# Start addresses in SBUF: y's parts and sums 64 bytes further on, Strassen's weights at offset 0, and w1's chunk behind a Strassen chunk at its usual place

## The chip, the cores and the metric

The kernel runs on one core of one Trainium2 chip. The metric is the device time of one execution in microseconds (us). Three executions of the kernel before took 2162.35, 2159.93 and 2165.89 us; the median is 2162.35 us.

## What is computed

A two-layer transformer on 256 tokens of width 2048, in float32. Layer 0 mixes with stick-breaking attention, layer 1 with a sparse attention of three branches; behind each stands an MLP with a squared ReLU. The parts that matter here:

```python
def sqrelu_mlp(h, w1, w2):
    return jnp.square(jax.nn.relu(h @ w1)) @ w2

def reference(x, ...):
    h = x
    for layer in range(DEPTH):                       # DEPTH = 2
        ...
        h = h + stick_breaking_attention(rms_norm(h, ...), sb_w_qkv[slot], sb_w_out[slot])   # layer 0
        h = h + native_sparse_attention(rms_norm(h, ...), nsa_w_in[slot], ...)               # layer 1
        h = h + sqrelu_mlp(rms_norm(h, mlp_norm_g[layer]), mlp_w1[layer], mlp_w2[layer])
```

`mlp_w1` is 2048 x 8192 and `mlp_w2` 8192 x 2048 in each layer.

## The kernel before, in words

**Arithmetic.** Every large product is made in float32r on TensorE, with each operand split into a high part (ScalarE, a copy that rounds) and a low part (VectorE, the difference). A product is the sum of three matmuls: high by high, low by high, high by low. A matmul has a stationary operand (128 x 128, loaded by a weight load that runs beside the matmul before it) and a moving operand of 256 or 512 columns.

**Three kinds of chunk.** Weights come from HBM in chunks of 128 x 1024 numbers.

- `chunk_T` (line 194) makes a transposed product for w1 and for q and k. Stationary: the weights. Moving: x, 256 columns. A chunk is 16 matmuls with the high weights (`acc<-xs,hi`, x's high and low part in turn) and 8 with the low weights (`acc<-xs,lo`), all at line 208.
- `chunk_N` (line 155) makes a product with tokens as rows: v, the attentions' outputs, part of w2. Stationary: x or y (y is the MLP's hidden layer, or the attention's result). Moving: the weights, 512 columns. A chunk is 12 matmuls at line 159.
- `chunk_S` (line 239) does a part of w2 by Strassen's scheme: 21 matmuls with 256 columns at line 275 in the place of 12 with 512. Stationary: y or its sums `ss`. Moving: three plain blocks of the weights (`shi`, `slo`) and four sums of blocks (`hi`, `lo` out of `ts`).

**Order.** In `mlp` the hidden layer is cut into four parts (`fg` 0 to 3). For each part `group1` (line 440) runs 4 x 8 = 32 chunks of w1, and `group2` (line 468) the chunks of w2 that take this part in. In `group1` of `fg` 1 to 3 the last output block of the part before is done by eight Strassen chunks, two in every eight w1 chunks: `then={2: step, 5: step}` puts one behind the third and one behind the sixth. `group2` has eight Strassen chunks of its own between its `chunk_N`. With two layers, there are 6 groups of the first kind with 8 Strassen chunks each, so 48 of these, and 8 groups of the second kind with 64 Strassen chunks. TensorE takes its instructions in the order in which the code makes them.

**Places.** Below, the *place* of an operand is its start address within a partition, modulo 256 bytes. By the built program's memory map the buffers of x's parts, y's parts, `ss`, the weights' `hi` and `lo` and Strassen's `shi` and `slo` all begin at place 128, and every slice that a matmul takes out of them is a multiple of 256 bytes further on. The code adds an offset (line 131, counted in 4-byte numbers) to some of them: `NEAR` 0, `FAR` 16, `TURN` 8, `SUM` 48, `SUM0` 60. That gives:

| operand | role | offset | place |
|---|---|---|---|
| x, in `chunk_T` | moving | none | 128 |
| w1, q, k weights, usual | stationary | FAR | 192 |
| w1 at the start of `group1` for `fg` > 0, all 24 matmuls | stationary | TURN | 160 |
| w1 in the chunk behind a Strassen chunk: first 14 matmuls, then 2 + 8 | stationary | TURN, then FAR | 160, then 192 |
| y, `ss` | stationary | none | 128 |
| weights in `chunk_N` | moving | NEAR | 128 |
| Strassen's `slo`, `hi`, `lo`; in `group1` `shi` too | moving | SUM | 64 |
| Strassen's `shi` in `group2` (first 6 matmuls) | moving | SUM0 | 112 |

The chunk behind a Strassen chunk is split by `split_turn` (line 181): ScalarE and VectorE each do it in two instructions (896 and 128 columns) that write to different offsets, where the usual `split` (line 133) takes one each.

Of the kernel before, what the change touches and what calls it, by code (L numbers as in the profile page):

```python
# [8 lines left out]
F32 = mybir.dt.float32  # L9
F32R = mybir.dt.float32r  # L10
AF = mybir.ActivationFunctionType
OP = mybir.AluOpType
# [3 lines left out]
P = 128  # L16
T = 256
NT = T // P
D = 2048
KD = D // P  # L20
NB = 512
# [4 lines left out]
KC = 2  # L26
# [15 lines left out]
def hybrid_kernel(  # L42
# [6 lines left out]
    nc = tc.nc  # L49
    cpool = ctx.enter_context(tc.tile_pool(name="cpool", bufs=1))  # L50
# [3 lines left out]
    whi = ctx.enter_context(tc.tile_pool(name="whi", bufs=4))  # L54
    wlo = ctx.enter_context(tc.tile_pool(name="wlo", bufs=4))
# [5 lines left out]
    h = cpool.tile([P, NT, D], F32, name="h")  # L61
    xs = cpool.tile([P, KD, 2, T], F32R, name="xs")
    xhi, xlo = xs[:, :, 0, :], xs[:, :, 1, :]
    yhi = cpool.tile([P, KD, T], F32R, name="yhi")
    ylo = cpool.tile([P, KD, T], F32R, name="ylo")


    G_SB, G_M0, G_M1, G_NSA, G_Q, G_K = 0, KD, 2 * KD, 3 * KD, 64, 65
# [39 lines left out]
    def pump():  # L108
        if beside:
            b = beside[0]  # L110
            b[2] += b[1] / KC
            while b[2] >= 1:
                b[2] -= 1
                y = next(b[0], b)
                if y is b:
                    beside.remove(b)
                if y:
                    break
# [8 lines left out]

    PAD = 64  # L130
    NEAR, FAR, TURN, SUM, SUM0 = 0, 16, 8, 48, 60

    def split(raw, o=(NEAR, NEAR)):
        n = KC * NB
        view = lambda t, a: t[:, a:a + n].rearrange("p (k n) -> p k n", k=raw.shape[1])
        hi = view(whi.tile([P, n + PAD], F32R, tag="hi", name="hi"), o[0])
        nc.scalar.activation(hi, raw, AF.Copy)  # L137
        lo = view(wlo.tile([P, n + PAD], F32R, tag="lo", name="lo"), o[1])
        nc.vector.tensor_tensor(lo, raw, hi.bitcast(F32), op=OP.subtract)  # L139
        return hi, lo  # L140

    def load(src, k0, nk, n0, nn):
        raw = wraw.tile([P, nk, nn], F32, tag="raw", name="raw")
        nc.sync.dma_start(
            raw, src[k0 * P:(k0 + nk) * P, n0:n0 + nn].rearrange("(k p) n -> p k n", p=P)
        )
        return raw

    def load_split(*where, o=(NEAR, NEAR)):
        return split(load(*where), o)  # L150
# [3 lines left out]

    def chunk_N(ps, src, k0, n0, first, last, ahi, alo, koff=0, by_token=False):

        hi, lo = src if isinstance(src, tuple) else load_split(src, k0, KC, n0, NB)
        tiles = [(kk, k0 - koff + kk, t) for kk in range(KC) for t in range(NT)]
        mm = lambda a, b, k, t, s, e: nc.tensor.matmul(ps[t], a[:, k, t * P:(t + 1) * P], b, start=s, stop=e)  # L159
        if by_token:  # L160

            half = [slice(0, NB // 2), slice(NB // 2, NB)]
            for t, c in [(0, slice(0, NB)), (1, half[0]), (1, half[1])]:
                for a, w in ((ahi, hi), (alo, hi), (ahi, lo)):
                    for kk in range(KC):
                        k = k0 - koff + kk
                        nc.tensor.matmul(
                            ps[t][:, c], a[:, k, t * P:(t + 1) * P], w[:, kk, c], start=False, stop=True,
                            skip_group_check=True,
                        )  # L170
            return
        for part in [tiles]:
            for kk, k, t in part:
                mm(ahi, hi[:, kk, :], k, t, first and kk == 0, False)
                mm(alo, hi[:, kk, :], k, t, False, False)
            pump()
            for kk, k, t in part:
                mm(ahi, lo[:, kk, :], k, t, False, last and kk == KC - 1)
            pump()

    def split_turn(raw):

        flat = raw.rearrange("p k n -> p (k n)")
        n, c = KC * NB, KC * NB - P
        h, l = whi.tile([P, n + PAD], F32R, tag="hi", name="hi"), wlo.tile([P, n + PAD], F32R, tag="lo", name="lo")
        for a, b, o in ((0, c, TURN), (c, n, FAR)):
            nc.scalar.activation(h[:, o + a:o + b], flat[:, a:b], AF.Copy)
            nc.vector.tensor_tensor(
                l[:, FAR + a:FAR + b], flat[:, a:b], h[:, o + a:o + b].bitcast(F32), op=OP.subtract
            )  # L190
        cut = lambda t, o: [t[:, o(j) + j * P:o(j) + (j + 1) * P] for j in range(n // P)]
        return cut(h, lambda j: TURN if (j + 1) * P <= c else FAR), cut(l, lambda j: FAR)

    def chunk_T(ps, src, k0, n0, first, last, nk=KC, o=(FAR, FAR)):

        nm = KC * NB // P // nk
        tiles = [(kk, m) for kk in range(nk) for m in range(nm)]
        if o is None:
            hi, lo = split_turn(load(src, k0, nk, n0, nm * P))
        else:  # L200
            hi, lo = [
                [w[:, kk, m * P:(m + 1) * P] for kk, m in tiles]
                for w in (src if isinstance(src, tuple) else load_split(src, k0, nk, n0, nm * P, o=o))
            ]

        def mm(w, x, kk, m, s, e):
            o = ps[m // 2][:, (m % 2) * T:(m % 2 + 1) * T]
            nc.tensor.matmul(o, w, x[:, k0 + kk, :], start=s, stop=e, skip_group_check=True)  # L208

        for (kk, m), w in zip(tiles, hi):  # L210
            mm(w, xhi, kk, m, first and kk == 0 and m % 2 == 0, False)
            mm(w, xlo, kk, m, False, False)
        pump()
        for (kk, m), w in zip(tiles, lo):
            mm(w, xhi, kk, m, False, last and kk == nk - 1)
        pump()

    def proj_T(ps, src, n0, nk=KC, turn=False, then={}):

        for i in range(KD // nk):  # L220
            k0 = i * nk
            o = (TURN, TURN) if turn and i == 0 else None if i - 1 in then else (FAR, FAR)
            chunk_T(ps, src, k0, n0, k0 == 0, k0 + nk == KD, nk, o)
            if i in then:
                then[i]()

    def proj_Th(src, n0):

        ps = bank(acc, "acc")
        proj_T([ps], src, n0, 2 * KC)  # L230
        return ps
# [7 lines left out]
    def chunk_S(ps, src, k0, n0, first, last, ahi, alo, shi, slo, koff=0, o=SUM0):  # L239
# [9 lines left out]
        hi, lo = [  # L249
            wsum.tile([P, 3 * W + PAD], F32R, tag=n, name=n, bufs=1)[:, a:a + 3 * W]  # L250
            for n, a in (("shi", o), ("slo", SUM))
# [57 lines left out]
    def proj_N(src, n0, pool=acc, tag="acc"):  # L309
        ps = [bank(pool, tag) for _ in range(NT)]  # L310
        for k0 in range(0, KD, KC):
            chunk_N(ps, src, k0, n0, k0 == 0, k0 + KC == KD, xhi, xlo)
        return ps
# [87 lines left out]
    def out_proj(src, layer, g0):  # L401

        ps = {nb: [bank(acc, "acc") for _ in range(NT)] for nb in (0, 1)}
        for nb in (0, 1):
            for k0 in range(0, KD - HG, KC):
                chunk_N(ps[nb], src, k0, nb * NB, k0 == 0, False, yhi, ylo)
        drain()
        for nb in range(D // NB):
            if nb < 2:
                k00 = KD - HG  # L410
            else:
                ps[nb] = [bank(acc, "acc") for _ in range(NT)]
                k00 = 0
            for k0 in range(k00, KD, KC):
                chunk_N(ps[nb], src, k0, nb * NB, k0 == 0, k0 + KC == KD, yhi, ylo)
            add_h(nb, ps[nb])
            spawn(next_x(layer, nb, g0), 1)

    def mlp(l, layer, junk, done, last=None):
        w1, w2 = mlp_w1[l], mlp_w2[l]  # L420
        ss = junk.tile([P, 2, KD // 2, 4, P], F32R, name="ss", bufs=1)
        row = junk.tile([P, T], F32, name="row", bufs=1)

        def rows():
# [271 lines left out]
    with tc.tile_pool(name="m0p", bufs=2) as mp:  # L696
        wsum = mp
        def done0(nb, pool):
            spawn(next_x("nsa", nb, G_NSA, pool), 1.5)

        mlp(0, "m0", mp, done0)
# [5 lines left out]
    with tc.tile_pool(name="nsa", bufs=2) as ap, ExitStack() as last:  # L707
# [298 lines left out]
        for k0 in range(0, KD, GK):  # L1006
            raw = load(w_in, k0, GK, D + 6 * NB + GATES - P, P)
# [6 lines left out]
            for kk in range(GK):  # L1014
                k = k0 + kk
# [40 lines left out]
        for g in range(G):  # L1056
            ps = [bank(acc, "acc") for _ in range(NT)]
            for k0 in range(0, KD, KC):
                raw = wraw.tile([P, KC, NB], F32, tag="raw", name="raw")
# [26 lines left out]
    with tc.tile_pool(name="m1p", bufs=2) as mp:  # L1086
        wsum = mp
        ov = out[0].rearrange("(t p) d -> p t d", p=P)

        def done1(nb, pool):  # L1090
            if nb < D // NB - 1:
                nc.sync.dma_start(ov[:, :, nb * NB:(nb + 1) * NB], h[:, :, nb * NB:(nb + 1) * NB])

        mlp(1, "m1", mp, done1, ov)
# [29 lines left out]
```

## Time and profile before

| | |
|---|---|
| median of three executions | 2162.35 us |
| the profiled execution, its own time | 2154.16 us |
| its span, first to last instruction | 2152.4 us |
| granted TensorE clock | 1.000 |
| VectorE busy, ScalarE busy | 1597.2 us, 1205.3 us |

The profile's groups list a kind of instruction by line and operands, with its count and mean duration. A matmul's duration there is that of one from its start to its modelled end; since matmuls are pipelined, these overlap, and the mean says little about the rate. The rate is read from the timeline: it merges equal instructions in a row into one line with the start of the first and their count, so the difference of two starts, divided by the count, is what one matmul costs.

### The profile page before, as it was taken

Reading aid. Unit: us, or ns where it says so; the run is one execution under the profiler, and the core shown is the slowest. Engines: PE = TensorE matmul, PEld = TensorE weight load, DVE = VectorE, ACT = ScalarE, POOL = GpSimd, SP = SyncE. Lnnn points to the kernel's source line nnn. Section 1 sums busy time; section 2 is a strip of 40 time slices with the busy share of each in tenths; the row PEclk is TensorE's granted clock in tenths of the full one; section 3 lists DMA queues with packets and bytes.
Section 4 is the critical chain, followed back from the end, with each engine's and each line's share of the span. In section 5 each row is a group of like instructions: output and inputs, shape, how many; then the busy total and the mean of one; then the engine's idle time right before and its main releaser. Section 6 shows DMA issues by size and latency. Waiting matters only on the chain.

```text
span 2152.4 us, 37355 instructions
## 1 busy us (share of the span) xinstructions
PE 2145.5 (100%) x14898; PEld 1983.1 (92%) x14898; DVE 1597.2 (74%) x2241; ACT 1205.3 (56%) x1639; POOL 42.6 (2%) x75
## 2 busy tenths in 40 slices
PE   9999999999999999999999999999999999999999
PEld 9999988998998999999898888889989989989998
DVE  5556556568878878878877888755778798788786
ACT  6555665555555555555556666654555555555553
POOL 0000000000000000000000011000000000000000
PEclk9999999999999999999999999999999999999999
DMA  7655555665665665765667654456656656656664
GB/s 240 210 168 176 158 181 177 184 201 188 206 195 187 206 196 187 225 195 184 202 178 225 173 144 135 145 168 188 193 196 199 194 188 215 199 183 206 196 198 164
DMA packets 260790, 406.35 MB, mean 189 GB/s; under 512 B 13188, under 2 KB 91912, under 8 KB 260616
## 3 DMA queue, kind: packets, MB, share of 16 engines
q1 hardware_dynamic: 259800, 403.52, 60.1%
q8 instruction: 116, 1.90, 0.3%
q14 instruction: 58, 0.48, 0.1%
q10 hardware_dynamic: 816, 0.46, 0.1%
HBM read 401.83 MB, written 2.10 MB: 188 GB/s over the span
## 4 chain that ended last, share of the span: by engine, by line
PE 99%; DVE 0%; POOL 0%; ACT 0%; issue 0%; DVEq 0%; ACTq 0%; POOLq 0%
PE acc L208 43%; PE acc L159 37%; PE att L275 13%; PE att L159 1%; PE att L332 1%; PE att L946 1%; PE att L612 0%; PE att L660 0%; PE att L884 0%; PE att L940 0%; PE att L886 0%; PE att L885 0%; PE att L939 0%; PE att L938 0%; PE att L862 0%; PE att L779 0%
## 5 line engine op out<-in xcount | busy, mean ns | idle before, releaser
L137 ACT ACTIVATE hi<-raw 128x1024 fp32r<-128x1024 f32 x591 | 624.7, 1059 | 509.2 <-PE acc L208 211.3
L139 DVE TENSOR_TENSOR lo<-raw,hi 128x1024 fp32r<-128x1024 f32 x591 | 719.7, 1221 | 244.9 <-ACT hi L137 227.0
L208 PE MATMUL acc<-xs,hi 128*128 128x256 f32 x5360 | 669.0, 277 | 0.0
L208 PEld LDWEIGHTS acc<-xs,hi 128*128 128x128 f32 x5360 | 638.7, 188 | 1.0
L208 PE MATMUL acc<-xs,lo 128*128 128x256 f32 x2680 | 359.6, 277 | 0.0
L208 PEld LDWEIGHTS acc<-xs,lo 128*128 128x128 f32 x2680 | 329.4, 188 | 0.0
L159 PE MATMUL acc<-hi,yhi 128*128 128x512 f32 x828 | 324.6, 392 | 0.0
L159 PE MATMUL acc<-hi,ylo 128*128 128x512 f32 x828 | 323.0, 390 | 0.0
L159 PE MATMUL acc<-lo,yhi 128*128 128x512 f32 x828 | 223.3, 391 | 0.0
L137 ACT ACTIVATE hi<-ts 128x1024 fp32r<-128x1024 f32 x112 | 118.8, 1061 | 178.5 <-DVE ts L255 98.0
L159 PEld LDWEIGHTS acc<-lo,yhi 128*128 128x128 f32 x828 | 154.6, 188 | 31.5
L159 PEld LDWEIGHTS acc<-hi,ylo 128*128 128x128 f32 x828 | 155.5, 188 | 29.6 <-DVE ylo L319 0.2
L159 PEld LDWEIGHTS acc<-hi,yhi 128*128 128x128 f32 x828 | 155.5, 188 | 29.6 <-ACT yhi L318 0.2
L159 PE MATMUL acc<-hi,xs 128*128 128x512 f32 x704 | 177.5, 392 | 0.0
L248 DVE TENSOR_TENSOR ts<-raw 128x512 f32<-128x512 f32 x112 | 77.1, 691 | 128.2 <-DMA raw<-in_mlp_w_dram 128.0
L159 PEld LDWEIGHTS acc<-hi,xs 128*128 128x128 f32 x704 | 130.1, 188 | 26.5 <-ACT hi L137 0.2
L139 DVE TENSOR_TENSOR lo<-ts,hi 128x1024 fp32r<-128x1024 f32 x112 | 136.6, 1220 | 9.4 <-ACT hi L137 9.0
L253 ACT ACTIVATE shi<-raw 128x768 fp32r<-128x768 f32 x112 | 94.5, 844 | 60.8 <-PE att L275 36.3
L256 DVE TENSOR_TENSOR slo<-raw,shi 128x768 fp32r<-128x768 f32 x112 | 106.6, 952 | 0.4 <-PE att L275 0.4
L159 PE MATMUL acc<-lo,xs 128*128 128x512 f32 x352 | 96.7, 395 | 0.0
L275 PE MATMUL att<-hi,ss 128*128 128x256 f32 x672 | 95.9, 279 | 0.0
L275 PEld LDWEIGHTS att<-hi,ss 128*128 128x128 f32 x672 | 86.4, 189 | 0.0
(251 smaller groups left out, 2246.0 us busy)
## 6 DMA issues: line engine op xcount, KB each, us to landing
raw<-in_mlp_w_dram SPq DMA_DIRECT2D x512, 512.0 KB, 4.4
raw<-in_sb_w_qkv_dram SPq DMA_DIRECT2D x95, 512.0 KB, 4.3
raw<-in_nsa_w_in_dram SPq DMA_DIRECT2D x50, 512.0 KB, 3.8
raw<-in_sb_w_out_dram SPq DMA_DIRECT2D x32, 512.0 KB, 3.9
raw<-in_nsa_w_in_dram SPq DMA_DIRECT2D x64, 256.0 KB, 3.4
raw<-in_nsa_w_out_dram SPq DMA_DIRECT2D x32, 512.0 KB, 3.6
w1t<-in_nsa_cmp_w_dram SPq DMA_DIRECT2D x8, 512.0 KB, 3.9
h<-in_x_dram SPq DMA_DIRECT2D x8, 256.0 KB, 4.4
```

The source lines that it names most:

```text
L137: nc.scalar.activation(hi, raw, AF.Copy)
L139: nc.vector.tensor_tensor(lo, raw, hi.bitcast(F32), op=OP.subtract)
L159: mm = lambda a, b, k, t, s, e: nc.tensor.matmul(ps[t], a[:, k, t * P:(t + 1) * P], b, start=s, stop=e)
L208: nc.tensor.matmul(o, w, x[:, k0 + kk, :], start=s, stop=e, skip_group_check=True)
L248: nc.vector.tensor_tensor(ts[:, :2, :], flat[:, W:3 * W].rearrange("p (a n) -> p a n", a=2), b12, op=OP.subtract)
L253: nc.scalar.activation(hi, flat[:, :3 * W], AF.Copy)
L256: nc.vector.tensor_tensor(lo, flat[:, :3 * W], hi.bitcast(F32), op=OP.subtract)
L275: nc.tensor.matmul(ps[i], a, w, start=s, stop=e, skip_group_check=True)
L332: nc.tensor.transpose(ps[:, j * T + t * P:j * T + (t + 1) * P], h[:, t, (kp + j) * P:(kp + j + 1) * P], ident)
L946: nc.tensor.transpose(ptp[:w, j * P:(j + 1) * P], src(j), ident)
```

## The change

The arithmetic and the order of TensorE's instructions stay the same. Four things differ:

- `yhi`, `ylo` and `ss` are allocated 64 numbers longer, and used from number 16 on: their place goes from 128 to 192.
- `chunk_N` puts its weights at `FAR` where y is the stationary operand (w2 and the two output projections): place 192 and no longer 128. Where x is, both stay at 128.
- `SUM` becomes 0 and `SUM0` 12: Strassen's weights lie at 128, and `shi` in `group2` at 176.
- `split_turn` is removed. The w1 chunk behind a Strassen chunk is split like the others, at `FAR`, place 192. The 24 matmuls at the start of `group1` (`turn`) keep `TURN`.

```diff
-    yhi = cpool.tile([P, KD, T], F32R, name="yhi")
-    ylo = cpool.tile([P, KD, T], F32R, name="ylo")
+    PAD, FAR = 64, 16
+
+    def far(pool, n, name):
+        return pool.tile([P, n + PAD], F32R, name=name, bufs=1)[:, FAR:FAR + n]
+
+    yhi, ylo = [far(cpool, KD * T, n).rearrange("p (k t) -> p k t", k=KD) for n in ("yhi", "ylo")]
...
-    PAD = 64
-    NEAR, FAR, TURN, SUM, SUM0 = 0, 16, 8, 48, 60
+    NEAR, TURN, SUM, SUM0 = 0, 8, 0, 12
...
-        hi, lo = src if isinstance(src, tuple) else load_split(src, k0, KC, n0, NB)
+        near = (FAR, FAR) if ahi is yhi else (NEAR, NEAR)
+        hi, lo = src if isinstance(src, tuple) else load_split(src, k0, KC, n0, NB, o=near)
...
-    def split_turn(raw):
...
-        if o is None:
-            hi, lo = split_turn(load(src, k0, nk, n0, nm * P))
...
-            o = (TURN, TURN) if turn and i == 0 else None if i - 1 in then else (FAR, FAR)
+            o = (TURN, TURN) if turn and i == 0 else (FAR, FAR)
...
-        ss = junk.tile([P, 2, KD // 2, 4, P], F32R, name="ss", bufs=1)
+        ss = far(junk, KD * 4 * P, "ss").rearrange("p (a k i n) -> p a k i n", a=2, k=KD // 2, i=4)
```

The instructions of TensorE stand in the same order in both programs, so none of its rows is shown. ScalarE and VectorE each have 48 instructions less. On ScalarE, at the first Strassen chunk that runs beside w1 (layer 0, `fg` 1), there stood before, with `raw` the chunk as it was loaded, `ts` the sums of a Strassen chunk and `uv` the end of the Strassen chunks ahead:

```order
L299 ACTIVATE uv<-att 128x256
L137 ACTIVATE hi<-ts 128x1024
L187 ACTIVATE hi<-raw 128x896
L187 ACTIVATE hi<-raw 128x128
L137 ACTIVATE hi<-raw 128x1024 x2
L253 ACTIVATE shi<-raw 128x768
```

At the same place now:

```order
L287 ACTIVATE uv<-att 128x256
L140 ACTIVATE hi<-ts 128x1024
L140 ACTIVATE hi<-raw 128x1024 x3
L241 ACTIVATE shi<-raw 128x768
```

The two halves of the chunk behind the Strassen chunk have become one instruction of the usual kind, and nothing has changed its turn. VectorE's halves (line 188) go the same way.

More of the change, by code (lines that the diff above doesn't have):

```diff
@@ L179, in chunk_N @@
             pump()
-    def split_turn(raw):
[L183 to L192, printed above, removed]
     def chunk_T(ps, src, k0, n0, first, last, nk=KC, o=(FAR, FAR)):
@@ L197, in chunk_T @@
         tiles = [(kk, m) for kk in range(nk) for m in range(nm)]
-        if o is None:
-            hi, lo = split_turn(load(src, k0, nk, n0, nm * P))
[L200 to L204, printed above, removed]
+        hi, lo = [
+            [w[:, kk, m * P:(m + 1) * P] for kk, m in tiles]
+            for w in (src if isinstance(src, tuple) else load_split(src, k0, nk, n0, nm * P, o=o))
+        ]
         def mm(w, x, kk, m, s, e):
```

## The prediction

> **What bounds the kernel now.** I read the page's head and chain first, then TensorE's waits, then its timeline, chunk by chunk.
>
> ```profile
> span 2152.4 us, 37355 instructions
> PE 2145.5 (100%) x14898; PEld 1983.1 (92%) x14898; DVE 1597.2 (74%) x2241; ACT 1205.3 (56%) x1639; POOL 42.6 (2%) x75
> PE 99%; DVE 0%; POOL 0%; ACT 0%; issue 0%; DVEq 0%; ACTq 0%; POOLq 0%
> PE att L520 <- POOL ident masks.py:199: 1.6, 1, 1.6
> PE att L791 <- DVE hs L786: 0.9, 1, 0.9
> PE acc L539 <- ACT hi L532: 0.4, 1, 0.4
> core 0: 2152.4 us, clock 1.000
> ```
>
> TensorE is busy throughout and is 99% of the chain that ended last; its three waits, all that the view of waits lists, come to 2.9 us; its clock is granted in full. So the time is the number of matmuls times what each costs, and the change leaves their number and order as they are. Only their cost can move.
>
> That cost is in the timeline of TensorE: columns are start, length, instruction, count. Here is a stretch of `group1` with one Strassen chunk (563.00 to 565.48) and the w1 chunks around it.
>
> ```profile
> 560.28 1.98 PE L208 MATMUL acc<-xs,hi 128*128 128x256 f32 x16
> 562.09 1.07 PE L208 MATMUL acc<-xs,lo 128*128 128x256 f32 x8
> 563.00 0.28 PE L275 MATMUL att<-shi,yhi 128*128 128x256 f32 x1
> ...
> 565.48 2.04 PE L208 MATMUL acc<-xs,hi 128*128 128x256 f32 x16
> 567.36 1.07 PE L208 MATMUL acc<-xs,lo 128*128 128x256 f32 x8
> ```
>
> - A usual w1 chunk, places 128 (moving) and 192 (stationary): 563.00 - 560.28 = 2.72 us for 24 matmuls, **113.3 ns** each.
> - The Strassen chunk, places 64 and 128: 565.48 - 563.00 = 2.48 us for 21 matmuls of the same 256 columns, **118.1 ns** each.
> - The 16 high matmuls behind it, 14 of them at place 160: 567.36 - 565.48 = 1.88 us, against 562.09 - 560.28 = 1.81 us in the usual chunk.
>
> The same Strassen matmuls, at the same places, run faster in `group2`:
>
> ```profile
> 489.23 0.39 PE L159 MATMUL acc<-hi,yhi 128*128 128x512 f32 x1
> ...
> 491.95 0.28 PE L275 MATMUL att<-shi,yhi 128*128 128x256 f32 x1
> ...
> 492.66 0.85 PE L275 MATMUL att<-hi,ss 128*128 128x256 f32 x6
> ...
> 494.36 0.39 PE L159 MATMUL acc<-hi,yhi 128*128 128x512 f32 x1
> ```
>
> There the six `shi` matmuls at place 112 take 492.66 - 491.95 = 0.71 us (118 ns each), and the 15 behind them, at 64 and 128 as in `group1`, take 494.36 - 492.66 = 1.70 us: 113.3 ns each. And the reverse: w1-like matmuls at their usual places, 128 and 192, run slowly where they stand directly behind a `chunk_N` at 128 and 128.
>
> ```profile
> 75.40 1.07 PE L159 MATMUL att<-lo,xs 128*128 128x512 f32 x4
> 76.30 2.05 PE L208 MATMUL acc<-xs,hi 128*128 128x256 f32 x16
> ...
> 79.13 2.05 PE L208 MATMUL acc<-xs,hi 128*128 128x256 f32 x16
> 81.01 1.11 PE L208 MATMUL acc<-xs,lo 128*128 128x256 f32 x8
> 81.96 0.60 PE L612 MATMUL att<-qT,kT 128*128 128x256 f32 x2
> ```
>
> Two chunks, 76.30 to 79.13 to 81.96, 2.83 us each: 117.9 ns a matmul, through to the end of the stretch. My reading: for one and the same pair of places there are two **levels**, 113.3 and 118 ns. A stream of matmuls keeps its level as long as its places stay the same, and a change of places can throw it from one to the other. Where `group1` goes from w1 to Strassen, both places fall by 64, the distance between them stays 64, and still the level is lost. So it is the step itself that costs, not where Strassen's operands lie.
>
> **The change part by part.**
>
> *Strassen in `group1`.* Moving operands go to 128, stationary ones to 192: exactly w1's. No step is left on the way in, on the way out, or within the chunk. If a level is held while places stay, these 21 matmuls go at w1's 113.3 ns, 2.38 us in the place of 2.48. 48 chunks x 0.10 = **4.8 us**.
>
> *The w1 chunk behind Strassen.* Place 160 goes; the chunk is like its neighbours: 1.88 becomes 1.81 us. 48 x 0.07 = **3.4 us**.
>
> *ScalarE and VectorE.* Each of the 48 chunks is split by one instruction and not by two:
>
> ```profile
> L137 ACT ACTIVATE hi<-raw 128x1024 fp32r<-128x1024 f32 x591 | 624.7, 1059 | 509.2 <-PE acc L208 211.3
> L187 ACT ACTIVATE hi<-raw 128x896 fp32r<-128x896 f32 x48 | 45.6, 949 | 20.5 <-PE acc L208 20.4
> L187 ACT ACTIVATE hi<-raw 128x128 fp32r<-128x128 f32 x48 | 14.1, 293 | 0.0
> L139 DVE TENSOR_TENSOR lo<-raw,hi 128x1024 fp32r<-128x1024 f32 x591 | 719.7, 1221 | 244.9 <-ACT hi L137 227.0
> L188 DVE TENSOR_TENSOR lo<-raw,hi 128x896 fp32r<-128x896 f32 x48 | 52.2, 1087 | 3.3 <-ACT hi L187 2.9
> L188 DVE TENSOR_TENSOR lo<-raw,hi 128x128 fp32r<-128x128 f32 x48 | 13.7, 285 | 0.0
> ```
>
> 949 + 293 - 1059 = 183 ns on ScalarE, 1087 + 285 - 1221 = 151 ns on VectorE, so 48 times 8.8 and 7.2 us less work. It gives nothing: both are ahead of TensorE, which waits for no weights. The busiest of these stretches shows that they can feed a TensorE that is 1.3 us faster:
>
> ```profile
> 544.00:651.00 107.00, 107.00 (x933) 106.99 (x932) 84.90 (x115) 57.98 (x67) 0.00 (x0) 1.00 0.62 197
> ```
>
> In a whole `group1` VectorE is busy 84.9 of 107 us and the DMA engines 0.62 of the time (the last columns are clock, DMA share and GB/s). Were that cover gone, a late chunk would cost TensorE part of the 1.2 us of a split; with 22 us of slack in a group I count nothing.
>
> *`chunk_N` with y.* Both operands move by 64, to 192 and 192. From the rows at 489.23 and 491.95, 12 matmuls take 2.72 us, 226.7 ns for 512 columns, which is the better level (113.3 for 256). A pair of places moved as one keeps both levels elsewhere: 64 and 128 has 113.3 and 118 as 128 and 192 has. I take no change. Bounds: from nothing to the first matmuls of a run, where the level has to be found; that is a fraction of a us a group.
>
> *Strassen in `group2`.* `shi` goes from 112 to 176, the rest from 64 to 128, y from 128 to 192, and the `chunk_N` around them from 128 to 192: all by 64. I take no change here either; if the six `shi` matmuls no longer lead to the better level, 64 x 15 x 4.5 ns = 4.3 us are lost, which is the bound. Below nothing there is at most the six at 118: 64 x 6 x 4.7 = 1.8 us.
>
> *The start of `group1`.* This is what I can't read off. Before, `chunk_N` at (128, 128) is followed by 24 matmuls at (128, 160) and then (128, 192):
>
> ```profile
> 543.10 1.08 PE L159 MATMUL acc<-lo,yhi 128*128 128x512 f32 x4
> 544.01 2.06 PE L208 MATMUL acc<-xs,hi 128*128 128x256 f32 x16
> 545.90 1.11 PE L208 MATMUL acc<-xs,lo 128*128 128x256 f32 x8
> 546.85 1.98 PE L208 MATMUL acc<-xs,hi 128*128 128x256 f32 x16
> 548.66 1.07 PE L208 MATMUL acc<-xs,lo 128*128 128x256 f32 x8
> ...
> 651.54 0.40 PE L159 MATMUL acc<-hi,yhi 128*128 128x512 f32 x1
> ```
>
> The 24 take 546.85 - 544.01 = 2.84 us (118.3 each), and at 546.85 the better level is there at once: 548.66 - 546.85 = 1.81. Now `chunk_N` ends at (192, 192), and its last matmul meets a weight load at 160 that is half as far on the other side. The 24 still stand between, but what they hand on may differ. I take the better level; the price of the other is a rival.
>
> *Sum.* 4.8 + 3.4 = 8.2 us; the rows are rounded to 0.01, so I make it once more over a whole group. From 544.01 to 651.54 (its first `chunk_N`) it takes 107.53 us, 32 w1 chunks and 8 of Strassen. With the 24 at 160 as now it would take 2.84 + 31 x 2.72 + 8 x 2.38 = 106.2: 1.33 less, and in 6 groups **8.0 us**, which I use. The profiled execution, 2154.16 us of its own (1.8 around its span), would come to 2146.2. It was faster than any of the three timed ones; against their median of 2162.35 the forecast is **2154.4 us**, 0.37% less.
>
> *A rule that speaks against it.* All of the 118 and 113.3 above are matmuls of one shape that differ in place and in what stood ahead alone. The Trainium skill (TensorE: Matmul & The Clock Gate, "Step-by-step: what each phase is for") says that TensorE has two independent SBUF read ports, so that loading the next tile's weights takes no read bandwidth from the running matmul. By that rule places give nothing and the sum is 0. The rows at 563.00 and 492.66 don't agree: the same operands, 118.1 and 113.3 ns.
>
> **The rivals.**
>
> 1. *`group1` starts on the wrong level (slower).* If the 24 matmuls at 160 hand on the 118 level, nothing in `group1` changes places any more, so nothing brings it back: the very steadiness that the change relies on holds the bad level for the whole group. Price: 31 chunks x 2.83 + 2.84 + 8 x 2.48 = 110.4 us, against 107.5 now; 2.9 x 6 groups = 17 us, to 2179. It decides by the first chunk behind the 24: 2.83 or 2.72. For it: the row at 76.30, where a `chunk_N` led to the bad level at these very places. Against: the six starts of today all end well, and so do 48 starts from Strassen, over the same place 160. If the groups differ, each that fails costs 2.9 + 1.3 = 4.2 against the forecast, so 2159 to 2175.
> 2. *Strassen still throws the level, now with nothing behind it to catch it (slower).* If what matters in `group1` isn't the step in place but, say, the other buffers, the chunk stays at 118 and w1 behind it too, until the group ends. Price as in 1, less the two or three chunks ahead of the first Strassen chunk: some 15 us, to 2177. Against it: in `group2` fifteen such matmuls run at 113.3 out of the same buffers.
> 3. *`group2` loses its 113.3* while `group1` gains: -8.0 + 4.3 = -3.7 us, 2158.6.
> 4. *Places count for nothing* and the levels have another cause: no change, 2162.35. The rule above would have it so; the rows speak against it.
>
> **How the numbers follow.** Forecast 0.60; rival 1 in all groups 0.16, in some 0.07; rival 2 0.06; rival 3 0.06; rival 4 0.05. Against the median, 0.3% is 6.5 us, about what a measurement of this kernel can tell from no change. The forecast's 8.0 is just beyond; with the spread of the timed runs (2159.93 to 2165.89) its own range is 2150 to 2158, and I count a fifth of it as "same". Faster: 0.60 x 0.8 = 0.48. Same: 0.12 + 0.06 + 0.05 + a part of the mixed case = 0.25. Slower: 0.16 + 0.06 + the rest of the mixed case = 0.27. Rivals 1 and 2 together hold more than 0.2, so the range has to reach to 2180; below it ends at the forecast's 2150.
>
> **What would show it.** In the timeline after: a Strassen chunk in `group1` from its first `shi` row to the next w1 row in 2.38 us (2.48 if step one is wrong); the 16 high matmuls behind it in 1.81 (1.88 or more if wrong); the first usual chunk behind a group's 24 in 2.72 (2.83 for rival 1); fifteen matmuls in `group2` still in 1.70 (1.77 for rival 3); the 12 of a `chunk_N` in 2.72. A whole `group1` then takes 106.2 us and not 107.5. New waits of TensorE for `hi` or `lo` would show that the cover was less than I count.

## The result, and the profile after

| us | median | lowest to highest | ratio to before, with its 95% interval |
|---|---|---|---|
| before, same set | 2160.84 | 2158.43 to 2165.89 | |
| after | 2170.86 | 2169.65 to 2172.27 | 1.0051 [1.0035, 1.0067] |

The changed kernel is slower by 10 us; 2154.4 was forecast. (One execution of after at 6945 us, and one of before at 9381 us in the set of e1 below, are left out of the spreads and ratios; no profile shows what held them up.) The profiled execution took 2169.65 us of its own against 2154.16 before.

These are the head of the page after and, from the view of waits, what TensorE waited for (total, times, longest):

```profile
span 2167.9 us, 37259 instructions
PE 2160.6 (100%) x14898; PEld 1998.4 (92%) x14898; DVE 1596.8 (74%) x2193; ACT 1200.8 (55%) x1591; POOL 42.6 (2%) x75
```

```profile
PE att L508 <- POOL ident masks.py:199: 1.6, 1, 1.6
PE att L779 <- DVE hs L774: 0.9, 1, 0.9
PE acc L527 <- ACT hi L520: 0.8, 1, 0.8
```

The same 14898 matmuls, the same three small waits, a span 15.5 us longer. So nothing waits for anything new: the matmuls themselves cost more. TensorE's timeline shows where, in the first `group1` with Strassen chunks (w1 is now line 196, Strassen 263, `chunk_N` 163):

```profile
542.53 1.08 PE L163 MATMUL acc<-lo,yhi 128*128 128x512 f32 x4
543.44 2.05 PE L196 MATMUL acc<-xs,hi 128*128 128x256 f32 x16
...
546.28 2.05 PE L196 MATMUL acc<-xs,hi 128*128 128x256 f32 x16
...
549.11 2.05 PE L196 MATMUL acc<-xs,hi 128*128 128x256 f32 x16
...
551.94 0.28 PE L263 MATMUL att<-shi,yhi 128*128 128x256 f32 x1
...
554.41 2.05 PE L196 MATMUL acc<-xs,hi 128*128 128x256 f32 x16
...
557.24 2.05 PE L196 MATMUL acc<-xs,hi 128*128 128x256 f32 x16
...
653.70 0.39 PE L163 MATMUL acc<-hi,yhi 128*128 128x512 f32 x1
```

The 24 matmuls at place 160 take 546.28 - 543.44 = 2.84 us, as before. The next chunk takes 549.11 - 546.28 = 2.83 us, where before it took 2.72: the better level is not found. From there on everything costs the same 117.8 ns a matmul: a Strassen chunk 554.41 - 551.94 = 2.47 us for 21, the w1 chunk behind it 2.83 for 24, and so to the end of the group. From 543.44 to 653.70 it takes 110.25 us by the trace's starts (before: 107.53), and the other five groups with Strassen chunks the same 110.25. 6 x 2.72 = 16.3 us, which is the whole of the 15.5 and 0.8 more.

Outside `group1` the levels are those of before. In `group2`, with y now at 192:

```profile
488.66 0.39 PE L163 MATMUL acc<-hi,yhi 128*128 128x512 f32 x1
...
491.38 0.28 PE L263 MATMUL att<-shi,yhi 128*128 128x256 f32 x1
...
492.09 0.85 PE L263 MATMUL att<-hi,ss 128*128 128x256 f32 x6
...
493.80 0.39 PE L163 MATMUL acc<-hi,yhi 128*128 128x512 f32 x1
```

12 matmuls of `chunk_N` in 2.72 us, six of `shi` in 0.71 and the fifteen behind them in 1.71, as before within the hundredth that the rows are rounded to.

### The profile page after: what moved, and what is told of

It is laid out like the page before. It is cut to its first block, busy times and chain, and to the rows that moved or that the text cites. A ratio compares the mean times of both kernels' runs of the same rounds, so it can differ in the third digit from the quotient of the medians.

```text
span 2167.9 us, 37259 instructions
## 1 busy us (share of the span) xinstructions
PE 2160.6 (100%) x14898; PEld 1998.4 (92%) x14898; DVE 1596.8 (74%) x2193; ACT 1200.8 (55%) x1591; POOL 42.6 (2%) x75
## 4 chain that ended last, share of the span: by engine, by line
PE 99%; DVE 0%; POOL 0%; ACT 0%; issue 0%; DVEq 0%; ACTq 0%; POOLq 0%
PE acc L196 43%; PE acc L163 37%; PE att L263 13%; PE att L163 1%; PE att L934 1%; PE att L320 1%; PE att L600 0%; PE att L648 0%; PE att L872 0%; PE att L928 0%; PE att L874 0%; PE att L873 0%; PE att L926 0%; PE att L927 0%; PE att L850 0%; PE att L767 0%
## 5 line engine op out<-in xcount | busy, mean ns | idle before, releaser
L140 ACT ACTIVATE hi<-raw 128x1024 fp32r<-128x1024 f32 x639 | 675.4, 1058 | 593.0 <-PE acc L196 288.2
L142 DVE TENSOR_TENSOR lo<-raw,hi 128x1024 fp32r<-128x1024 f32 x639 | 778.5, 1221 | 284.8 <-ACT hi L140 266.7
L196 PE MATMUL acc<-xs,hi 128*128 128x256 f32 x5360 | 678.9, 279 | 0.0
L196 PEld LDWEIGHTS acc<-xs,hi 128*128 128x128 f32 x5360 | 647.3, 189 | 1.0
L196 PE MATMUL acc<-xs,lo 128*128 128x256 f32 x2680 | 366.1, 279 | 0.0
L196 PEld LDWEIGHTS acc<-xs,lo 128*128 128x128 f32 x2680 | 335.7, 189 | 0.0
L140 ACT ACTIVATE hi<-ts 128x1024 fp32r<-128x1024 f32 x112 | 118.6, 1059 | 141.6 <-DVE ts L243 61.3
```

## The experiments

**Is it the start of the group alone?** Theory A, formed from these rows, is that of rival 1: what the 24 matmuls at 160 hand on holds for the group. If a start that hands on the better level is put in, the rest of the forecast should come true. The trace gave the place to cut. These are the differences of neighbouring starts, in ns, from the group's first matmul on; the bars mark the turns of a rhythm:

```
before  118 118 119 119 120 117 118 116 | 122 116 116 120 116 123 117 117 | 122 115 116 120 117 122 118 116 | then 114 113
after   121 116 119 118 116 | 122 116 116 120 116 123 117 117 | 122 116 115 120 117 123 117 117 | 121 116 116 | then 119 118
```

At 160 a rhythm of eight matmuls sets in (122 116 116 120 116 123 117 117, 947 ns together). Before, it began at the ninth matmul, so that the step to 192 came after two full turns of it. After, with y and `chunk_N`'s weights at other places ahead, it begins at the sixth, and the step comes three matmuls into a turn. So 21 at 160 in the place of 24 would again end on a full turn:

```diff
+    def split_turn(raw, nh, nl):
...
+        hat = lambda j: (TURN if j < nh else FAR) + j * P
...
+        lat = lambda j: (TURN if j < nl else FAR) + j * P
...
-                proj_T(ps, w1, fg * D + fb * NB, turn=fg > 0 and fb == 0,
+                proj_T(ps, w1, fg * D + fb * NB, turn=21 if fg > 0 and fb == 0 else 0,
```

Here `split_turn` serves the first w1 chunk of a group alone: all 16 high matmuls and the first five low ones read their weights at 160, the rest at 192.

> The changed kernel, but at the start of group1 (fg 1 to 3) only 21 of the 24 matmuls stand at place 160 (all 16 high ones and the first 5 low ones); the last 3 low ones stand at 192. Theory A (the level is handed on: the matmuls at 160 go through a rhythm of eight, and the level that follows depends on where in it they end; today they end 3 matmuls behind the row of 122 ns, in the kernel before they ended right where that row would have come): at 21 they end where the next 122 would come, the first usual w1 chunk takes 2.72 us, every group1 106.2 us in the place of 110.25, and the span is 2167.9 - 6 x 4.05 = 2143.6 us. Theory B (at the new places, behind a chunk_N at 192 or beside Strassen at 128, these matmuls simply cost 118 ns): group1 stays at 110.2 us and the span at 2168.

It took 2149.34 us against 2155.41 for before in the same set, ratio 0.9968 [0.9955, 0.998], and is faster than both kernels. Its timeline at the same place (w1 is line 216, Strassen 283):

```profile
544.15 2.05 PE L216 MATMUL acc<-xs,hi 128*128 128x256 f32 x16
...
546.97 1.98 PE L216 MATMUL acc<-xs,hi 128*128 128x256 f32 x16
...
549.69 1.98 PE L216 MATMUL acc<-xs,hi 128*128 128x256 f32 x16
...
552.41 0.28 PE L283 MATMUL att<-shi,yhi 128*128 128x256 f32 x1
...
554.79 1.98 PE L216 MATMUL acc<-xs,hi 128*128 128x256 f32 x16
...
557.51 1.98 PE L216 MATMUL acc<-xs,hi 128*128 128x256 f32 x16
```

The chunk behind the start takes 2.72 us, the Strassen chunk 554.79 - 552.41 = 2.38 and the w1 chunk behind it 2.72. All six groups take 106.18 us; on TensorE nothing but the places of three weight tiles separates them from the 110.25 of after. The span missed the expectation, 2148.4 against 2143.6, and the view of waits has a good part of the reason:

```profile
PE att L283 <- DVE slo L264: 2.8, 3, 2.0
```

TensorE waits for Strassen's weights in `group2`; the same view shows no such wait in before's profile or in after's. The view counts idle time behind a matmul's modelled end alone. Start against start with after, four Strassen chunks of `group2` are late by 3.6 us together, and 0.7 us more comes ahead of the first such `group1`. The longest such wait, on VectorE's timeline and then on TensorE's:

```profile
2096.27 0.69 DVE L256 TENSOR_TENSOR ts<-raw 128x512 f32<-128x512 f32 x1 [1.87 <-DMA raw<-in_mlp_w_dram]
...
2098.93 0.95 DVE L264 TENSOR_TENSOR slo<-raw,shi 128x768 fp32r<-128x768 f32 x1
```

```profile
2099.93 0.50 PE L283 MATMUL att<-slo,yhi 128*128 128x256 f32 x2 [2.03 <-DVE slo L264]
```

VectorE stands idle for 1.87 us for a chunk of weights that is still on its way, and TensorE for 2.03 us behind it. Part of what `group1` gained is given back here in waits for loads.

**Which counts end well?** The same kernel with a count of its own in each of the six groups:

```diff
+                proj_T(..., turn=((17, 18, 19), (20, 22, 23))[l][fg - 1] if fg > 0 and fb == 0 else 0,
```

> The changed kernel with another number of matmuls at 160 at the start of each of the six group1: 17, 18, 19 in layer 0 and 20, 22, 23 in layer 1. Theory A: each group is at one of two lengths, 106.2 or 110.2 us, decided by its number alone; with all of these away from the good point of the rhythm, at least half of them are at 110.2. Theory B: all six at 110.2 us.

Only two groups failed, so "at least half" missed; that there are two lengths and nothing between them held. With these six and the two known counts I read the rule off: the rhythm starts behind the fifth matmul, so n matmuls end (n - 5) mod 8 into a turn. 0, 1, 4, 5 and 6 had ended on the better level (21; 22; 17; 18; 19), 2, 3 and 7 on the other (23; 24; 20). That rule was then tried on counts it had not seen. Up to 16, `split_turn` cuts among the high matmuls, and all low ones stand at 192:

```diff
+                proj_T(..., turn=((8, 10, 12), (14, 16, 6))[l][fg - 1] if fg > 0 and fb == 0 else 0,
```

> The changed kernel with yet other numbers of matmuls at 160 at the start of the six group1: 8, 10, 12 in layer 0 and 14, 16, 6 in layer 1. The map so far: 20, 23 and 24 end at 118 ns, 17, 18, 19, 21 and 22 at 113. If what counts is the place in a rhythm of eight (theory A), a number ends as the one eight or sixteen above it: 8 and 16 as 24 (118, group 110.2 us), 12 as 20 (118, 110.2), 10 as 18 (113, 106.2), 14 and 6 as 22 (113, 106.2). If it is chance or anything else about the count (theory C), the six don't follow this; three of six would by luck.

All six came out as the rule has them. Lengths of `group1` in us, both runs and the two other kernels together:

| into a turn | 0 | 1 | 2 | 3 | 4 | 5 | 6 | 7 |
|---|---|---|---|---|---|---|---|---|
| count n | 21 | 6, 14, 22 | 23 | 8, 16, 24 | 17 | 10, 18 | 19 | 12, 20 |
| us | 106.18 | 106.12, 106.16, 106.20 | 110.25 | 110.24, 110.25, 110.25 | 106.18 | 106.12, 106.16 | 106.19 | 110.25, 110.25 |

A group's fate rests on the length of what runs at 160, and a longer run at 160 does no good of itself. Two groups of one execution, n = 10 and n = 12 (w1 is line 215):

```profile
717.00 2.02 PE L215 MATMUL acc<-xs,hi 128*128 128x256 f32 x16
718.86 1.07 PE L215 MATMUL acc<-xs,lo 128*128 128x256 f32 x8
719.76 1.98 PE L215 MATMUL acc<-xs,hi 128*128 128x256 f32 x16
...
886.36 2.05 PE L215 MATMUL acc<-xs,hi 128*128 128x256 f32 x16
888.25 1.10 PE L215 MATMUL acc<-xs,lo 128*128 128x256 f32 x8
889.19 2.05 PE L215 MATMUL acc<-xs,hi 128*128 128x256 f32 x16
```

The first eight low matmuls, all at (128, 192) in both, take 0.90 and 0.94 us.

**Can the start do without 160?** A rival to A was that the better level is found by whatever breaks the stream, as the attention's own matmuls do in before's trace (behind the `att<-qT,kT` from 81.96 on, the same w1-like matmuls that ran at 117.9 ns ahead of it are at 113.3 from 86.00). Here nothing lies at 160, and two transposes of the identity stand ahead of the group's first w1 matmul (they write a bank that w1 then begins anew):

```diff
+                if fg > 0 and fb == 0:
+                    for j in range(2):
+                        nc.tensor.transpose(ps[0][:, j * P:(j + 1) * P], ident, ident)
+                proj_T(ps, w1, fg * D + fb * NB,
```

> The changed kernel without any matmul at 160; instead two transposes of the identity stand ahead of the first w1 matmul of group1 (fg 1 to 3), into a bank that this matmul overwrites. All places of w1 and Strassen are those of the changed kernel. Theory A: transposes ahead of w1 led to 113 ns in all 13 cases of the trace of before, so each group1 takes 106.1 us plus some 0.4 for the transposes, span about 2146 us. Theory B (the places cost it): 110.2 us and 2168.

The expectation fell: 2163.45 us, ratio 1.0037 [1.0023, 1.0051], and groups of 110.32, 106.18, 110.32, 106.17, 110.32 and 110.32 us. But it shows most plainly that places alone don't decide. The first and the second group have the same instructions at the same places:

```profile
543.66 2.13 PE L196 MATMUL acc<-xs,hi 128*128 128x256 f32 x16
545.62 1.11 PE L196 MATMUL acc<-xs,lo 128*128 128x256 f32 x8
546.57 2.05 PE L196 MATMUL acc<-xs,hi 128*128 128x256 f32 x16
...
717.08 2.08 PE L196 MATMUL acc<-xs,hi 128*128 128x256 f32 x16
719.00 1.07 PE L196 MATMUL acc<-xs,lo 128*128 128x256 f32 x8
719.90 1.98 PE L196 MATMUL acc<-xs,hi 128*128 128x256 f32 x16
```

The eight low matmuls behind the first sixteen take 0.95 us in the first and 0.90 in the second, and so it stays. A start without a run at 160 lands on either level. Before's trace holds a case of this that the expectation left out: behind a smaller transpose (64 x 64) at 392.32, w1 runs at some 118 ns a matmul.

**Are before's 107.53 an accident of one execution?** The kernel before, unchanged, profiled again:

> The kernel before once more, for a second profile: its profiled execution was 6.7 us faster than the median of its timed ones, the changed kernel's was 1.2 us faster. If the level at a group's start is decided anew in each execution, one or more of the six group1 take about 110.3 us here in the place of 107.53; if it is fixed by the program, all six take 107.53 and the 6.7 us lie elsewhere.

Six groups of 107.53 us again. Its own time was 2156.34, 2.2 us over the first profile, with 1.3 us of waits for `slo` in `group2` that the first profile lacked. In these two executions the level is fixed by the program; start against start, what differs between them is 2.4 us in `group2`, most of it where `slo` came late.

**The parts of the change one by one**, each on the kernel before. First the chunk behind Strassen at its usual place, and no more:

```diff
-            o = (TURN, TURN) if turn and i == 0 else None if i - 1 in then else (FAR, FAR)
+            o = (TURN, TURN) if turn and i == 0 else (FAR, FAR)
```

> The kernel before with one part of the change alone: split_turn goes, w1 behind a Strassen chunk of group1 stands at 192 at once; y stays at 128 and Strassen at 64. Strassen there still takes 2.48 us. By theory A w1 behind it gets one level or the other and holds it to the next Strassen chunk: a group1 takes 2.84 + 2 x 2.72 + 29 x 2.83 + 8 x 2.48 = 110.2 us if that is 118 ns, 107.53 - 8 x 0.07 = 107.0 if it is 113. I expect the first, so 6 x 2.7 = 16 us more than before. If places alone set the cost (theory B), 107.0, and 3.4 us less than before.

2165.75 us, ratio 1.0044 [1.0029, 1.0058]; groups of 109.53. The part on w1 held, the length did not:

```profile
549.78 1.98 PE L208 MATMUL acc<-xs,hi 128*128 128x256 f32 x16
...
552.50 0.28 PE L275 MATMUL att<-shi,yhi 128*128 128x256 f32 x1
...
554.98 2.05 PE L208 MATMUL acc<-xs,hi 128*128 128x256 f32 x16
...
560.63 2.05 PE L208 MATMUL acc<-xs,hi 128*128 128x256 f32 x16
...
563.46 0.29 PE L275 MATMUL att<-shi,yhi 128*128 128x256 f32 x1
...
565.86 2.04 PE L208 MATMUL acc<-xs,hi 128*128 128x256 f32 x16
```

The first Strassen chunk, entered from w1 at 113.3 ns, runs at 118 (2.48 us) and leaves w1 behind it at 117.8 (2.83 us a chunk). The second, entered from that level, takes 2.40 us, 114.4 ns, and w1 behind it is at 117.8 once more. The 14 matmuls at 160 that the change takes out had been a repair, worth 2 us a group.

Then Strassen's weights at 0, and no more:

```diff
-    NEAR, FAR, TURN, SUM, SUM0 = 0, 16, 8, 48, 60
+    NEAR, FAR, TURN, SUM, SUM0 = 0, 16, 8, 0, 12
```

> The kernel before with Strassen's weights moved alone: SUM 0 and SUM0 12, so they lie at 128 (shi in group2 at 176), against y and its sums at 128 as before. Moving and stationary operand then begin at the same place; the first chunk of the kernel has such matmuls with 256 columns, at 120 ns. Expected: Strassen in group1 21 x 120 = 2.52 us, the 15 in group2 1.80 us, together 48 x 0.04 + 64 x 0.10 = 8.3 us more than before, if w1 behind is caught by its 14 matmuls at 160 as before; up to 16 us more where it isn't. By the reading that only a step between neighbours costs, group1's Strassen at 128 would be no step for the moving operand, and at 113.

2165.35 us (one execution, as for the next), groups of 107.91: with both operands at 128 Strassen's matmuls take 119.9 ns in `group1`, and the fifteen in `group2` 119.8, as expected. That only a step between neighbours costs, by which the expectation had them at 113 in `group1`, falls. Last, y, the sums and `chunk_N`'s weights moved, and Strassen's weights left at 64:

```diff
+    yhi, ylo = [far(cpool, KD * T, n).rearrange("p (k t) -> p k t", k=KD) for n in ("yhi", "ylo")]
...
+        hi, lo = ... load_split(src, k0, KC, n0, NB, o=(FAR, FAR) if ahi is yhi else (NEAR, NEAR))
...
+        ss = far(junk, KD * 4 * P, "ss").rearrange("p (a k i n) -> p a k i n", a=2, k=KD // 2, i=4)
```

> The kernel before with y, its sums and the weights of chunk_N behind y moved alone, to 192; Strassen's weights stay at 64 (112), split_turn stays. chunk_N with 512 columns: no change, 2.72 us for 12 (theory A, a pair moved as one). Strassen has 64 and 192, a distance of 128 that no trace shows: between 113 and 120 ns, so its 21 take 2.38 to 2.52 us. The starts of group1 are those of the changed kernel (192, then 160), so with 24 matmuls at 160 the first two w1 chunks are at 2.83 us, until the 14 at 160 behind the first Strassen chunk set the level anew.

2162.12 us, groups of 107.88. Strassen at (64, 192) takes 118.6 to 119.9 ns in `group1`, within the 113 to 120 that were expected, and the start comes out as expected too. It shows which part of the change spoiled it:

```profile
544.73 2.05 PE L211 MATMUL acc<-xs,hi 128*128 128x256 f32 x16
...
547.57 2.05 PE L211 MATMUL acc<-xs,hi 128*128 128x256 f32 x16
...
555.74 2.04 PE L211 MATMUL acc<-xs,hi 128*128 128x256 f32 x16
...
558.52 1.98 PE L211 MATMUL acc<-xs,hi 128*128 128x256 f32 x16
```

The first usual chunk is at 2.05 us for its sixteen, as in after: moving y and `chunk_N`'s weights ahead of the 24 is enough; which of the two does it, no run separates. But the 14 matmuls at 160 in the chunk from 555.74 bring the level back (1.98 at 558.52). In e7, where y stays, the 24 end well as before.

**A shorter start that ends well**, 10 at 160 in all groups (the edit of e5 with `turn=10`), and after once more beside it on one chip:

> The changed kernel with 10 of the 24 matmuls at 160 at every start of group1. In the rhythm this is the middle of three numbers that all end at 113 ns (as 17, 18, 19). Theory A: all six group1 at 106.1 us, 4.1 less than in the changed kernel each, and 1.4 less than in the kernel before; timed, 6 to 8 us faster than the kernel before, as with 21. Were the level decided anew in each execution, one or more would be at 110.2.

> The changed kernel once more, timed beside the others. Its six group1 are 6 x 2.72 = 16.3 us longer than those of the kernel before, the timed difference was 10.0. If the starts of group1 are fixed by the program, all six are at 110.25 again. If the rest is waits for loads that the kernel before has and the slower one hasn't, the profile shows none of TensorE's waits for slo or hi in group2, and the timed difference is again under 16, between 9 and 15 us.

The kernel with 10 took 2148.44 us, ratio 0.9968 [0.9958, 0.9978], with all groups at 106.12: no better than 21 beyond the intervals, and faster than both kernels again. Its profiled execution was its longest, 2156.62 us, and the view of waits shows:

```profile
PE att L282 <- DVE slo L263: 5.9, 5, 2.3
...
PE att L282 <- DVE lo L142: 1.3, 2, 0.8
```

These are 7.2 us of waits for Strassen's weights in `group2`, in a run 8.2 us over the median; start against start, its `group2` are 11.4 us longer than after's, so a run at the median seems to have some of this too. After took 2170.55, ratio 1.0071 [1.0058, 1.0084], all groups at 110.25, and no such wait. 15.9 us over before's 2154.69 is a little more than the 9 to 15 that I expected, and what the profiles give (15.5).

## Why the prediction was wrong

**The step that failed** is "The start of `group1`": "The 24 still stand between, but what they hand on may differ. I take the better level". They hand on the other, in all six groups: with y and `chunk_N`'s weights moved, the rhythm at 160 begins at the sixth matmul and not at the ninth, and 24 then ends three matmuls into a turn (e8 shows the start spoiled by this part of the change alone, e1 shows it mended by the count alone). Why the rhythm begins earlier, and why it has eight matmuls, stays open. It is rival 1, by its own sign (the first chunk behind the 24 in 2.83 us) and nearly by its price: 110.4 us a group and 17 us were worked out, 110.25 and 16.3 came. I gave it 0.16. What I counted against it weighed less than it seemed. "The six starts of today all end well" is close to one case: in every program here with one count at 160 for all groups, the six ended alike. The 48 starts from Strassen have 14 matmuls at 160 and not 24, and 14 ended well in e5 too. And the row at 76.30 did not stand alone: in before's trace four more starts behind a `chunk_N` with nothing at 160 (at 149.18, 222.05, 1080.09 and 1463.49) run at 117.8 ns.

**The terms of the sum were right**, once the start is mended: Strassen in `group1` 2.38 us a chunk, w1 behind it 2.72, a whole group 106.2 (e1: 106.18). Rival 2 is settled by this: at w1's places Strassen's matmuls hold the level they are given, good or bad. But "it is the step itself that costs, not where Strassen's operands lie" was too strong: at (128, 128) they take 119.9 ns in e7, in `group1` and in `group2`, slower than either level, so where they lie counts too.

**"I count nothing" for the cover was too good.** Of the 8.0 us, e1 and e9 give 6.1 and 6.3 in timed medians; lowest against lowest they give 8.3 (2153.55 and 2145.23) and 8.0 (2153.74 and 2145.71), the whole sum. Their profiles show the kind of cost that lies between: 2.8 and 7.2 us of waits for `slo` and `lo` in `group2`, behind loads. The 22 us of slack were read in a `group1`, and there they hold. The stretch that a faster `group1` runs into has no part in the prediction; in before's first such `group2` VectorE (the third busy time) has 9 us of 64 to spare:

```profile
651.00:715.00 64.00, 64.00 (x372) 56.37 (x371) 55.05 (x73) 35.97 (x37) 0.00 (x0) 1.00 0.61 198
```

**Right as predicted:** `chunk_N` at (192, 192) still takes 2.72 us for 12, the fifteen Strassen matmuls of `group2` still 1.7, and the 96 instructions less on ScalarE and VectorE change no wait of TensorE. **Rival 4 falls:** the same matmuls take 106.2 or 110.25 us a group by the count at 160 alone. The Trainium skill (TensorE: Matmul & The Clock Gate, "Step-by-step: what each phase is for") states two independent SBUF read ports, one for the moving operand and one for the weight load. That places then give nothing, as the prediction drew from it, these 106.2 and 110.25 us do not bear out. Where in the chip the places act, no run here shows.

**The size, timed:** +10.0 us in the first set, +15.9 in the last. After stands at 2170.5 to 2170.9 in both; it is before that moved, 2160.84 and 2154.69. Loads that come late for `group2` would do that, as in e4 and e9, and a slower `group1` hides them in after; but no profile of an execution of before as long as those of the first set exists, so this is argued and not shown.

## What to carry to other kernels

Where a matmul's cost depends on what ran before it, a change that steadies a stream also steadies its worst state: ask first what state the stream is started in, and put a start there whose outcome is known, or several, one to a group, in one run. Equal outcomes in a loop count for little more than one observation; look for a second history. Read the cover of a saving where the faster engine arrives next, not only where the saving is made.

## What the runs showed of the hardware

- One matmul of 128 x 128 by 256 columns in float32r, with its weight load beside it, costs 113.3, 117.8 or 119.9 ns in steady streams, at a granted clock of 1.000. At places 128 and 192 either of the first two holds, by what ran ahead, and each held for the 912 matmuls behind the 24 of a group (113.3 in e1, 117.8 in after). At equal places (128, 128) the 21 of Strassen took 119.9, while 512 columns at equal places took 226.7 (twice 113.3).
- The steady lengths are whole multiples of 6.667 ns or close to them: 113.3 = 17 of them, 353.3 for three matmuls at the 117.8 level = 53, 946 to 947 for the eight of the rhythm at 160 near 142 (946.7), 119.9 near 18 (120.0). In before's trace the starts of all 76 stretches of 30 or more matmuls at 113.3 ns, at places 128 and 192 and from 11 to 2063 us, lie at one and the same point of that period, to about 0.2 ns once a drift of 1.6 ns in a ms is taken out. Strassen's fifteen in `group2` at 64 and 128 have a point of their own, some 1.7 ns off: a quarter of the period, as 64 is a quarter of 256. In after's trace, where they stand at 128 and 192, they have w1's point, to 0.3 ns. So the cost of a matmul seems to hang on where its start falls in a clock of 6.667 ns, at a point that goes with its places, and a run at 160 would move its start along; this is argued, and what in the chip has this period, no run here shows.
